# Channel transforms, norms and turns in the Fourier layer of a two-layer encoder, and the place of a small copy in its attention layer

## The chip, the cores and the metric

One core of a Trainium2 chip runs the whole program. The metric is the device time of one execution in microseconds; lower is better. Before the change the median of 3 runs is 1605.82 us (1604.63 to 1607.87).

## The reference

Two token sequences (2048 and 512 rows of 1024 channels, float32) go through the same trunk: an attention layer, a Fourier layer, a final norm.

```python
def attention_layer(x, g, w_in, w_out, sink, rel_bias):
    h = rmsnorm(x, g)
    z = h @ w_in                       # q (16 heads of 64), k and v (4 heads), gate
    ...
    o = banded_gqa_with_sink(q, k, v, rel_bias, sink)   # |i-j| <= 128, bias by distance, a sink logit per head
    return x + (o * jax.nn.silu(gate)) @ w_out

def fourier_layer(x, g, w_gate, w_out):
    h = rmsnorm(x, g)
    hg = h.reshape(b, s, 4, 256)
    f = jnp.fft.fftn(hg, axes=(1, 3), norm="ortho").real   # over positions and the 256 channels of a group
    gate = h @ w_gate
    return x + (f.reshape(b, s, d) * jax.nn.silu(gate)) @ w_out
```

The result is `rmsnorm(x, final_norm)`.

## The kernel before

Products are made in float32 by splitting each operand into a high part (a value in the matmul's reduced format) and a low part (the rest): `matmul3` (line 94 in the profile) issues three matmuls, high by high, high by low, low by high. Where one operand is exact in its high part, two matmuls do. A split is a copy on ScalarE and a subtraction, on VectorE or on POOL. POOL cannot read the matmuls' accumulators (PSUM), so it only works on tiles in SBUF, and does so in pieces of 256 columns.

**Order.** The program is written in Python as straight code; a planner turns it into one fixed list of instructions for each engine, by priority (the order in the program) and by its own estimate of when inputs are ready and buffers free. Each engine then runs its list in order, and waits on semaphores. `seq(engine, ins)` chains instructions of an engine in the order written. Each pool of tiles has a fixed number of buffers (`bufs`), and a tile waits until a buffer is free.

**Attention** (`attention_phase`) runs over five chunks of 512 tokens, in each over eight head pairs `p`, two blocks of 128 queries at a time (17 steps `n`, the work of step `n` overlapping the rest of step `n-1`). In the first chunk the weights are split on the way (lines 113 and 118); later chunks load them split. A head pair's bias tile `bt` has 386 columns: the middle 384 come by a DMA from `rowd` (line 426), the two end columns are the sink logits, copied by ScalarE (line 431). Both are issued in `start()`, at an even step, for the head pair that comes two steps later. `biased` (line 470, VectorE) adds the tile to the scores, `exps` (478, ScalarE) makes the exponentials, `transp` (509) transposes the weights on TensorE, `parts` (517 on ScalarE, 518 on VectorE) splits them, `av` (535) multiplies them with the values, and `out_evac` (544, 553, 555, 558, 559) applies the gate.

**Fourier layer, first part.** Token tiles of 128 rows are taken in ten pairs (`Pair`). For a pair, `load` brings two tiles from memory (line 959), `norms` multiplies each by its inverse root mean square and by the weight `gb` (line 964), where `sumsq` makes the squares on ScalarE (939), the mean on VectorE (87) and the power on POOL (88). `turn` transposes on TensorE: `turn(i, hf)` gives the four blocks of tile `i` with even (`hf` 0) or odd half of each channel group in one PSUM bank, `self.ps[i, hf]`, and mostly splits it (`own`, lines 979 and 980) into `A[i, hf]`. Then two things are computed from a pair.

The gate (`gates`): a product of the 256 tokens with `w_gate` by seven products in place of eight (Strassen's way, Winograd's form), with sums `F[1]` to `F[4]` of the operands (`sums`, lines 995 and 1002), split into `S[1]` to `S[4]` (`parts`, 913 and 914). In order: `W` = A[0,0] B11, `X` by quarters in between, `Z` = S[1] T1, `W` + S[2] T2, `Z` + S[4] B22, `W` + S[3] T3, `W` + A[1,1] N4. Between them stand the reads of the accumulators (`c11`, `c12`, `c22`; VectorE's additions are lines 1105, 1110, 1114), and `hook(0)` to `hook(6)`, where steps of the next pair are put in.

The channel transform, a DFT over the 256 channels of a group, once for each tile of a pair. For tile 1 (`z_odd_even`, line 1036) the table's symmetry is used: even outputs need the sum of the two halves of a group, which is `F[1]`, odd ones their difference, made in PSUM by `odd` (line 986). So a group takes two contractions of 128 rows with 128 columns of the table; both parts of the table stand side by side, so that a matmul has 256 columns: 16 matmuls, evacuated by ScalarE (1043) and VectorE (1044), which adds the two parts. For tile 0 (`z`, `matmul3` at line 94) the whole table is used: 24 matmuls of 256 columns in two banks, evacuated by ScalarE (1022). After every second pair `combine` runs six sums over the four tiles, a radix-4 step over positions (`radix4`, line 1135, VectorE, both operands in SBUF), and POOL stores the results (1198); they are made while the next pair's products run.

Before the first pair the weights `T1`, `T2`, `B11`, `B22` are split and its tiles normalised, between the last steps of the attention layer; `build` splits `N4` and `T3` after its transforms. Buffers: the tag `x` has 4 (one holds the table `chan_sb` throughout; the others serve the tiles `x1`, the sums `F` by twos, and `c`), the tag `hT` 8 (the splits), PSUM 5 banks `bank` (transposes and transforms) and 3 `acc` (products).

**Second part.** The DFT over positions, the gate, the output product (`Outs`, also by seven products, with weights `T1`, `T2`, `T3`, `N4`), and the final norm. For each of the last three frequencies `split_g` is called after the first product and `transform` after the second.

## Time and profile before

| | us |
|---|---|
| median of 3 runs | 1605.82 |
| the runs | 1604.63 to 1607.87 |
| the profiled execution | 1608.11 |
| its span | 1606.3 |
| busy: TensorE | 1586.9 |
| busy: VectorE | 1141.7 |
| busy: ScalarE | 880.3 |
| busy: POOL | 438.2 |

The attention layer lasts until 1076 us, the pairs of the Fourier layer from there to about 1345 us, the second part to the end. PE is TensorE's matmuls, PEld its weight loads, DVE is VectorE, ACT ScalarE, SP the engine that issues most DMAs. A row of a timeline gives the start, the duration, engine, line, operation, output and inputs, count, and in brackets the idle time before it and what ended that. A row of groups ends in busy time, mean nanoseconds of one, and idle time before it. A row of waits gives the engine and line that waited, for whom, the total, the count and the longest. A row of windows gives the length, then the busy time of PE, PEld, DVE, ACT and POOL with the number of instructions, the granted clock, the share of the DMA engines and GB/s.

### The profile page before, as it was taken

What the parts mean: (1) busy time and instruction counts of PE and PEld (TensorE: products, weight loads), DVE (VectorE), ACT (ScalarE), POOL (GpSimd) and SP (SyncE); (2) the same over time, 40 slices, a digit from 0 to 9 for tenths busy, and PEclk for the clock granted to TensorE, in tenths of its full rate; (3) what the DMA queues carried; (4) which work ended last, traced back from release to release, by engine and by line L of the source; (5) the groups of instructions that cost most, each with busy time, mean ns of one, the idle gap of its engine ahead of it and who ended that gap; (6) DMA issues with size and microseconds to landing.
All of it is one profiled execution on the core that took longest, in us unless ns stands there. A gap on an engine that the chain in (4) does not pass through costs nothing.

```text
span 1606.3 us, 27426 instructions
## 1 busy us (share of the span) xinstructions
PE 1586.9 (99%) x9755; PEld 1322.6 (82%) x9755; DVE 1141.7 (71%) x2779; ACT 880.3 (55%) x2107; POOL 438.2 (27%) x605
## 2 busy tenths in 40 slices
PE   9999999999999999999999999999999999999998
PEld 7776888888898888988888888878888887888886
DVE  6787665777538776377764577668878877888696
ACT  6687634677237674257752476646655554343352
POOL 2466561421403414024222242211112121100010
PEclk9999999999999999999999999999999999999999
DMA  7577696655765576756659656656657569455952
GB/s 291 207 286 263 226 349 233 227 220 205 289 230 191 206 257 235 251 194 229 238 164 334 211 208 222 243 201 225 217 203 248 184 224 407 166 185 206 352 192 92
DMA packets 100580, 373.90 MB, mean 233 GB/s; under 512 B 12139, under 2 KB 22379, under 8 KB 83036
## 3 DMA queue, kind: packets, MB, share of 16 engines
q1 hardware_dynamic: 81708, 297.91, 52.4%
q0 software_dynamic: 16400, 70.04, 11.3%
q10 hardware_dynamic: 2336, 4.20, 0.7%
q8 instruction: 78, 1.28, 0.3%
q14 instruction: 58, 0.48, 0.1%
HBM read 280.84 MB, written 91.26 MB: 232 GB/s over the span
## 4 chain that ended last, share of the span: by engine, by line
PE 83%; DMA 7%; DVE 5%; ACT 2%; issue 1%; POOL 1%; SPq 0%; POOLq 0%; DVEq 0%; ACTq 0%
PE qp L94 13%; PE gp L94 12%; PE op L94 9%; PE spt L94 8%; PE spt L451 6%; PE av L535 6%; PE W L94 5%; PE fo L94 4%; PE vp L94 4%; PE pt L509 3%; PE Z L94 3%; PE Wo L94 2%; PE X L94 1%; PE z L94 1%; DMA b<-rowd 1%
## 5 line engine op out<-in xcount | busy, mean ns | idle before, releaser
L470 DVE CUSTOM_DVE_ANT_0 S<-spt,b 128x385 f32<-128x385 f32 (+1 forms) x315 | 154.2, 528 | 121.1 <-PE spt L451 120.8
L94 PE MATMUL qp<-h,wq 128*128 128x512 f32 x960 | 238.6, 398 | 0.0
L94 PE MATMUL gp<-h,wg 128*128 128x512 f32 x960 | 237.4, 395 | 0.0
L94 PEld LDWEIGHTS gp<-h,wg 128*128 128x128 f32 x960 | 174.9, 188 | 43.3 <-issue 9.7
L94 PEld LDWEIGHTS qp<-h,wq 128*128 128x128 f32 x960 | 175.9, 189 | 41.8 <-issue 5.5
L478 ACT ACTIVATE S<-S 128x385 f32<-128x385 f32 (+1 forms) x320 | 190.3, 606 | 18.4 <-DVE S L470 17.0
L517 ACT CAST pts<-pt 128x384 fp32r<-128x384 f32 (+1 forms) x320 | 123.8, 472 | 131.1 <-PE pt L509 130.8
L518 DVE TENSOR_TENSOR pts<-pt,pts 128x384 fp32r<-128x384 f32 (+1 forms) x320 | 147.6, 523 | 34.5 <-ACT pts L517 33.6
L94 PE MATMUL op<-wo,uT 128*128 128x512 f32 x600 | 140.4, 391 | 0.0
L94 PE MATMUL fo<-wo,tTu 128*128 128x512 f32 x576 | 139.1, 392 | 0.0
L94 PEld LDWEIGHTS op<-wo,uT 128*128 128x128 f32 x600 | 111.9, 188 | 23.9 <-issue 0.7
L451 PE MATMUL spt<-kwin,qab 64*128 64x384 f32 (+1 forms) x945 | 129.5, 356 | 0.0
L559 POOL TENSOR_TENSOR uT<-o,uT 128x256 fp32r<-128x256 f32 x75 | 55.6, 741 | 250.5 <-ACT uT L558 246.2
L94 PEld LDWEIGHTS fo<-wo,tTu 128*128 128x128 f32 x576 | 106.3, 188 | 20.3
L535 PEld LDWEIGHTS av<-pts,v 128*128 128x128 f32 x576 | 101.0, 188 | 24.0 <-ACT pts L517 3.7
L535 PE MATMUL av<-pts,v 128*128 128x512 f32 (+1 forms) x576 | 117.0, 342 | 3.3 <-ACT pts L517 2.6
L451 PEld LDWEIGHTS spt<-kwin,qab 64*128 64x128 f32 x945 | 84.2, 185 | 29.9 <-issue 21.5
L490 DVE TENSOR_SCALAR S<-S 128x384 f32<-128x384 f32 (+1 forms) x192 | 91.4, 476 | 6.4
L555 POOL TENSOR_TENSOR o<-o,s 128x256 f32<-128x256 f32 x75 | 55.3, 738 | 134.4 <-DVE o L553 134.1
L94 PE MATMUL spt<-wo,uT 128*128 128x512 f32 x360 | 86.7, 392 | 0.0
L94 PEld LDWEIGHTS spt<-wo,uT 128*128 128x128 f32 x360 | 66.5, 188 | 13.7
L509 PEld LDWEIGHTS pt<-ident,S 64*128 64x128 f32 x1792 | 68.2, 138 | 5.2 <-issue 2.3
(317 smaller groups left out, 2985.8 us busy)
## 6 DMA issues: line engine op xcount, KB each, us to landing
wo<-wsd SPq DMA_DIRECT2D x32, 1024.0 KB, 5.9
wq<-wsd SPq DMA_DIRECT2D x31, 1024.0 KB, 7.6
wg<-wsd SPq DMA_DIRECT2D x31, 1024.0 KB, 5.1
x<-x1d SPq DMA_DIRECT2D x40, 512.0 KB, 3.7
b<-b21d SPq DMA_DIRECT2D x40, 512.0 KB, 6.5
b<-rowd SPq DMA_DIRECT2D x40, 384.0 KB, 4.3
xs<-in_x_dram SPq DMA_DIRECT2D x23, 512.0 KB, 6.7
s2d<-gt POOLq DMA_DIRECT2D x40, 256.0 KB, 3.2
```

Source lines behind the costliest of these rows:

```text
L94: pe(PE.matmul(out, a[i], b[j], start=start and i + j == 0, stop=stop and i == 1, skip_group_check=more))
L451: pe(PE.matmul(banks[j][:, 2 + k0 * P : 2 + k1 * P], res["q"][rows, qp, b * P : (b + 1) * P], kwin[g][rows, kp, b * P + k0 * P : b * P + k ...
L470: seq(DVE, DVE.tensor_tensor_reduce(out=s[:, e0:e1], in0=ps[:, 1 + e0 : 1 + e1], in1=st["bias"][:, j, 386 - e1 : 386 - e0][:, ::-1], scale ...
L478: last_exp[0] = seq(ACT, ACT.activation(s[:, e0:e1], s[:, e0:e1], AF.Exp, bias=s[:, 386:387], scale=-1.0, accum_out=s[:, 387:388]))
L490: seq(DVE, DVE.tensor_scalar(s[:, ks], s[:, ks], den, None, ALU.mult))
L509: pe(PE.transpose(ps[h][:, kb, j, :], ss[j][rows, 1 + kb * P : 1 + (kb + 1) * P], ident[rows, rows]))
L517: seq(ACT, ACT.copy(hi, ps[:, k0:k1]))
L518: seq(DVE, DVE.tensor_tensor(lo, ps[:, k0:k1], f32(hi), ALU.subtract))
L535: pe(PE.matmul(to, v, pt, start=n == part == 0, stop=part == 1 and n in (1, len(todo) - 1), skip_group_check=n > 1,))
L555: eng.tensor_tensor(o, o, s, ALU.mult)
L559: low = eng.tensor_tensor(lo, o, f32(hi), ALU.subtract)
```

## The change

Four things, and a small fifth.

- Both tiles of a pair are transformed the even and odd way (`z(i)`, first tile 1, then tile 0). For tile 0 the new `mix(0)` makes the sum of its two halves (`both`, in the free half of the pair's buffer of sums), splits it into `M[0, 0]` on ScalarE and POOL, and makes the difference in PSUM, split by `own` into `M[0, 1]`. `mix(1)` is what `odd` was. The table is kept for one half of the rows only.
- `norms` scales on ScalarE and multiplies by the weight on POOL in four pieces, in place of one instruction on VectorE.
- The turns of the next pair are put in a product later: `turns1` after the third product, `turns2` after the fourth, `turns3` and `turns4` after the fifth.
- The end columns of the bias tile are copied in a step of their own, `sinks()`, at the end of the odd step before the head pair's first.
- The loads of `N4` in the second part are issued in `transform`, not in `split_g`.

```diff
                     st["bias"] = bt
...
+                def sinks():
+                    ends = ACT.copy(
+                        st["bias"][:, :, 0:386:385], sk[:, 2 * p : 2 * p + 2, None].to_broadcast([P, 2, 2])
+                    )
+                    if p:
+                        seq(ACT, ends)
...
                 at[0].start()
+                at[0].sinks()
...
                     for i in range(4 * n, 4 * n + 4):
                         extra(i)
+                    if n % 2 and n < 15:
+                        at[n // 2 + 1].sinks()
...
                 def norms(self, i):
                     xt = self.x[i]
                     inv = sumsq(xt, f"b{self.ts[i]}")
-                    DVE.scalar_tensor_tensor(xt, xt, inv[:, 0:1], gb, ALU.mult, ALU.mult)
+                    ACT.activation(xt, xt, AF.Copy, scale=inv[:, 0:1])
+                    for j in range(4):
+                        cs = slice(j * 256, j * 256 + 256)
+                        POOL.tensor_tensor(xt[:, cs], xt[:, cs], gb[:, cs], ALU.mult)
...
-                def odd(self):
-                    ps = self.ps[1, 1]
-                    DVE.scalar_tensor_tensor(ps, ps, -2.0, self.F[1], ALU.mult, ALU.add)
-                    self.diff = self.own(ps, f"d{self.n}")
+                def mix(self, i):
+                    ps = self.ps[i, 1]
+                    if i:
+                        both = self.F[1]
+                    else:
+                        both = self.pair[:, 1]
+                        ACT.copy(both, self.ps[0, 0])
+                        DVE.tensor_tensor(both, both, ps, ALU.add)
+                        t = htile([P, 2, 512], F32R, f"tM{self.n}")
+                        ACT.copy(t[:, 0], both)
+                        for j in range(2):
+                            cs = slice(j * 256, j * 256 + 256)
+                            POOL.tensor_tensor(t[:, 1, cs], both[:, cs], f32(t[:, 0, cs]), ALU.subtract)
+                        self.M[0, 0] = t[:, 0], t[:, 1]
+                    DVE.scalar_tensor_tensor(ps, ps, -2.0, both, ALU.mult, ALU.add)
+                    self.M[i, 1] = self.own(ps, f"d{self.n}_{i}")
...
-                def z(self, hf):
-                    ...
-                            matmul3(
-                                ps[:, gg * 256 : gg * 256 + 256], (a[0][:, gs], a[1][:, gs]),
-                                (ch[:, kk, 0], ch[:, kk, 1]), kk == 0, kk == 1,
-                            )
-                    ...
-                def z_odd_even(self):
-                    t = self.ts[1]
+                def z(self, i):
+                    t = self.ts[i]
                     ...
                     for g in range(4):
                         ps = bank(f"z{t}_{g}")
-                        for odd, m in enumerate((self.S[1], self.diff)):
+                        for odd in range(2):
+                            m = self.M[i, odd]
                             to = ps[:, odd * 256 : odd * 256 + 256].rearrange("p (a n) -> p a n", a=2)
                             for part in range(2):
                                 PE.matmul(
-                                    to, m[part][:, g * P : (g + 1) * P], ch[:, 0, :, odd * P : (odd + 1) * P],
+                                    to, m[part][:, g * P : (g + 1) * P], ch[:, :, odd * P : (odd + 1) * P],
                                     start=part == 0, stop=part == 1,
                                 )
...
             def turns2(pr):
                 ...
                 pr.sums(4)
+                pr.mix(0)
                 pr.parts(2)
...
                 gates(pr, {
-                    1: [lambda: turns1(nx)], 2: [lambda: turns2(nx)], 3: [lambda: turns3(nx)], 4: [lambda: turns4(nx)],
-                    5: [lambda: nx.z_odd_even()],
-                    6: [lambda: nx.z(0), lambda: nx.z(1), lambda: combine(nx)],
+                    2: [lambda: turns1(nx)], 3: [lambda: turns2(nx)], 4: [lambda: turns3(nx), lambda: turns4(nx)],
+                    5: [lambda: nx.z(1)],
+                    6: [lambda: nx.z(0), lambda: combine(nx)],
                 })
...
                 def split_g():
                     nxt["s"] = [gated(name, r, xtile) for r in tiles]
-                    if not ft["N4"]:
-                        f_sums("N4", left)
                     nxt["p"] = [halves_of(name, *gl, hf) for hf in range(2)]
...
                 def transform(third):
+                    if not ft["N4"]:
+                        f_sums("N4", left)
```

More of the change, by code (lines that the diff above doesn't have):

```diff
@@ L429, in start @@
                     )
-                    ends = ACT.copy(bt[:, :, 0:386:385], sk[:, 2 * p : 2 * p + 2, None].to_broadcast([P, 2, 2]))
-                    if p:
-                        seq(ACT, ends)
                     st["bias"] = bt
@@ L565, in out_evac @@
                     return split
-                return start, scores, biased, exps, divide, transp, parts, av, out_evac
+                return start, sinks, scores, biased, exps, divide, transp, parts, av, out_evac
             def out_proj(c, uTs):
@@ L628, in out_proj @@
                 return steps
-            Heads = namedtuple("Heads", "start scores biased exps divide transp parts av out_evac")
+            Heads = namedtuple("Heads", "start sinks scores biased exps divide transp parts av out_evac")
             def pieces(out, a, b, op):
@@ L727, in even_odd @@
                 def even_odd():
-                    t = ready["chan"] = xtile([P, 2, 2, 256], F32R, "chan_sb")
+                    t = ready["chan"] = xtile([P, 2, 256], F32R, "chan_sb")
                     src = ready["table"].rearrange("p (a n o) -> p o a n", a=2, o=2)
-                    for kk in range(2):
-                        for odd in range(2):
-                            seq(ACT, ACT.activation(
-                                t[:, kk, :, odd * P : (odd + 1) * P], src[:, odd], AF.Copy, scale=-1.0 if kk and odd else 1.0
-                            ))
+                    for odd in range(2):
+                        seq(ACT, ACT.copy(t[:, :, odd * P : (odd + 1) * P], src[:, odd]))
                 def rows(i):
@@ L1170, in turns1 @@
                 pr.sums(1)
-                pr.odd()
+                pr.mix(1)
             def turns2(pr):
@@ L1611, in split_g, with transform @@
                     nxt["s"] = [gated(name, r, xtile) for r in tiles]
+                    nxt["p"] = [halves_of(name, *gl, hf) for hf in range(2)]
+                def transform(third):
                     if not ft["N4"]:
                         f_sums("N4", left)
-                    nxt["p"] = [halves_of(name, *gl, hf) for hf in range(2)]
-                def transform(third):
                     nxt["o"] = Outs(k1, position(name, k1, None, None, tiles, (nxt["s"], tb), nxt["p"], third))
```

26 lines of the change are left out of this document (8 added, 18 removed).

## The prediction

> **What bounds the kernel now.** I read the page first (busy times, then the 40 slices), after it the timeline of TensorE in the stretch that the change touches, the waits, and the busy time by windows.
>
> ```profile
> PE 1586.9 (99%) x9755; PEld 1322.6 (82%) x9755; DVE 1141.7 (71%) x2779; ACT 880.3 (55%) x2107; POOL 438.2 (27%) x605
> ```
>
> TensorE is busy almost throughout, but such a busy time also covers stretched matmuls, so I look at starts. Here is one pair of the Fourier layer, products and channel transforms:
>
> ```profile
> 1156.58 0.40 PE L1036 MATMUL z<-chan_sb,S 128*128 128x256 f32 x2
> ...
> 1158.49 2.91 PE L94 MATMUL W<-wN,tTb 128*128 128x512 f32 x12
> 1161.24 3.04 PE L94 MATMUL z<-chan_sb,tTb 128*128 128x256 f32 x24
> 1164.11 2.91 PE L94 MATMUL W<-wB,tTb 128*128 128x512 f32 x12
> ```
>
> A product of 12 matmuls takes 1161.24 - 1158.49 = 2.75 us from start to start, 0.23 us a matmul. The second tile's transform (line 1036, 16 matmuls) takes 1158.49 - 1156.58 = 1.91, the first tile's (line 94, 24 matmuls) 1164.11 - 1161.24 = 2.87; both are 0.12 us a matmul. TensorE's whole waiting from 1139 to 1320 us, seven pairs, is one row:
>
> ```profile
> PE z L94 <- DVE z L1044: 0.3, 1, 0.3
> ```
>
> So this stretch is bound by what TensorE issues, and a matmul less there is time less as long as the other engines keep up. How near they are (first window: the first two pairs; second: a pair without the sums of the radix-4 step, line 1135; third: one with them):
>
> ```profile
> core 0: us, PE busy (x) PEld busy (x) DVE busy (x) ACT busy (x) POOL busy (x), PEclk, DMA share, GB/s
> 1076.00:1113.20 37.20, 34.97 (x199) 30.50 (x198) 31.57 (x55) 26.09 (x51) 4.52 (x9) 0.95 0.70 242
> 1138.40:1164.10 25.70, 25.70 (x142) 22.25 (x141) 18.76 (x33) 14.95 (x29) 4.62 (x9) 1.00 0.55 197
> 1164.10:1190.40 26.30, 25.95 (x143) 22.30 (x142) 23.50 (x34) 13.79 (x27) 5.35 (x10) 1.00 0.76 267
> ```
>
> VectorE is the second in line: 2.8 us free in a radix pair, 6.9 in the other, and full at the start, where TensorE idles about 2 us.
>
> **Part 1, transforms.** The first tile's 24 matmuls become 16, as the second tile's are already: 2.87 - 1.91 = 0.96 us less in each of 10 pairs, **-9.6 us**, all on the engine that sets the end.
>
> What the others pay for it, and for the moved norms, by these rows:
>
> ```profile
> L964 DVE SCALAR_TENSOR_TENSOR x<-x,invb,g1b 128x1024 f32<-128x1024 f32 x16 | 20.5, 1284 | 8.3 <-POOL invb L88 7.7
> L939 ACT ACTIVATE jkb<-x 128x1024 bf16<-128x1024 f32 x16 | 16.9, 1056 | 9.9 <-DMA x<-x1d 9.9
> ...
> L1044 DVE SCALAR_TENSOR_TENSOR z<-z,z 128x256 f32<-128x256 f32 x32 | 11.5, 416 | 0.0
> L1002 DVE TENSOR_TENSOR s<-trb,s 128x512 f32<-128x512 f32 x16 | 10.9, 682 | 0.0
> ...
> L995 ACT COPY s<-trb 128x512 f32<-128x512 f32 x16 | 9.7, 608 | 0.2 <-PE trb L972 0.2
> L986 DVE SCALAR_TENSOR_TENSOR trb<-trb,s 128x512 f32<-128x512 f32 x8 | 5.6, 699 | 0.2
> ```
>
> ```profile
> L637 POOL TENSOR_TENSOR e<-w32e,e 128x256 fp32r<-128x256 f32 x48 | 34.4, 738 | 33.1 <-ACT e L693 33.1
> ```
>
> VectorE, per pair: two norm multiplies go (-2.57); the even-odd mix of the first tile brings an add (0.68), a subtract in PSUM (0.70) and the low part of the difference (about 0.69), and four evacuations (4 x 0.42 = 1.66): net +1.16. A radix pair then has 24.7 of 25.3 us, the other 19.9 of 24.7. ScalarE: two scalings of about 1.06, three copies of about 0.61 and 0.3 for smaller evacuations, +4.2 on 14.4: not a bound. POOL: 8 multiply pieces and 2 subtract pieces of 0.74, +7.4 on 5. So by busy time alone everything fits under TensorE's shorter pair. I cost it at nothing there, and price separately what the order and the ports can do.
>
> **Part 2, norms and turns.** A tile's norm loses a 1.28 us step and gains 1.06 (ScalarE) and four pieces, 4 x 0.74 = 2.95 us: 2.7 us longer. Its transposes move one product (2.75 us) back, which pays for exactly that. But the loads of the next tiles wait for buffers that the turns free, so they come 2.7 us later, and the second one up to 3.4 us more, since the mix holds its buffer (ScalarE 0.61, VectorE 0.68, ScalarE 0.61, POOL 1.5). The rows of a radix pair and the pair before it:
>
> ```profile
> 1156.10 0.69 DVE L1110 TENSOR_TENSOR c<-c,W 128x512 f32<-128x512 f32 x1 [0.45 <-PE W L94]
> ...
> 1163.91 1.28 DVE L964 SCALAR_TENSOR_TENSOR x<-x,invb,g1b 128x1024 f32<-128x1024 f32 x1
> 1165.10 1.22 DVE L1135 TENSOR_TENSOR er<-z,z 128x1024 f32<-128x1024 f32 x1
> ...
> 1170.26 1.03 PE L972 MATMUL trb<-ident,x 128*128 128x128 f32 x8
> 1171.39 1.23 DVE L1135 TENSOR_TENSOR er<-er,z 128x1024 f32<-128x1024 f32 x1
> 1173.88 1.03 PE L972 MATMUL trb<-ident,x 128*128 128x128 f32 x8
> ```
>
> The later tile's norm ends at 1165.19 and its transposes are at 1173.88: 8.7 us of slack, of which 8.7 - 2.7 - 3.4 - 2.7 + 2.75 = 2.6 is left. Enough, if POOL isn't held up. That is the doubt: the 8 multiply pieces now fall just where VectorE does the six 1.22 us sums of line 1135 (1165.10 to 1172.62), and both read two operands from SBUF. What then happens is seen where line 211 (VectorE, two SBUF operands) meets POOL's line 206:
>
> ```profile
> 422.52 6.65 POOL L206 TENSOR_TENSOR xk<-xk,invb 128x640 f32<-128x640 f32 x4
> ...
> 424.87 1.28 DVE L211 SCALAR_TENSOR_TENSOR h<-xk,g0s,h 128x512 fp32r<-128x512 f32 x1 [3.21 <-ACT h L210]
> ...
> 429.90 0.74 DVE L211 SCALAR_TENSOR_TENSOR h<-xk,g0s,h 128x512 fp32r<-128x512 f32 x1
> ```
>
> ```profile
> 637.99 6.15 POOL L206 TENSOR_TENSOR xk<-xk,invb 128x640 f32<-128x640 f32 x4
> 640.36 4.34 DVE L211 SCALAR_TENSOR_TENSOR h<-xk,g0s,h 128x512 fp32r<-128x512 f32 x1 [3.02 <-ACT h L210]
> ```
>
> The same instruction takes 0.74 us beside an idle POOL, 1.28 when it gets in after the POOL instruction under way, and 4.34 when POOL's row of four runs through. I take the milder case, which is the commoner in the trace: each sum waits for one piece, 6 x 0.74 = 4.4 us on VectorE. Of this, 1.5 is covered because the turns come later: the last sum ends at 1172.62, the new turn would be at 1170.26 + 2.75 and wants VectorE about 1.1 later, at 1174.1. Another 1.7 is covered because the sum of line 1110 ends at 1156.79 and the product that overwrites what it reads starts at 1158.49. What comes through is 4.4 - 1.5 - 1.7 = 1.2 us, in the four radix pairs that also have norms: **+4.8 us**. Bounds: nothing, or the 24 us of the second rival.
>
> On this the Trainium skill, "SBUF — State Buffer", section "Who interferes with whom", says that VectorE with two SBUF inputs and a POOL instruction that reads SBUF exclude each other for a whole instruction, and that the loser waits rather than slows. By that rule a sum waits for one piece and the term is the 4.8 above; the 4.34 row shows more than one instruction's wait, so there the measurement decides.
>
> **Part 3, the first two pairs.** VectorE is full there: 31.57 busy in a window in which TensorE stands still for about 2 us. Two mixes and eight evacuations bring 2 x 2.07 + 8 x 0.42 = 7.5 us, two norms take off 2.6: 36.5 us of work in 37.2 - 1.9 = 35.3. So the 1.9 saved is not had in full: **+1.6 us** (1.2, and 0.4 as an estimate for pieces that meet two-operand splits; between 0 and 4).
>
> **Part 4, sink columns.** ScalarE writes the end columns of the bias tile behind the bias load, which it overlaps, and waits:
>
> ```profile
> ACT b L431 <- DMA b<-rowd: 55.6, 32, 4.5
> ```
>
> Queued behind it are the casts of the transposed weights (line 517), which TensorE's product with the values needs. Mostly TensorE has other work. In the first chunk twice it has not:
>
> ```profile
> 132.54 0.51 PE L535 MATMUL av<-pts,v 128*128 128x512 f32 x1 [0.81 <-ACT pts L517]
> ...
> 134.36 2.89 PE L94 MATMUL qp<-h,wq 128*128 128x512 f32 x12
> ...
> 139.07 0.56 PE L509 MATMUL pt<-ident,S 64*128 64x64 f32 x11 [0.80 <-DVE o L553]
> ...
> 151.10 0.20 ACT L431 COPY b<-sk 128x4 f32<-128x4 f32 x1 [4.49 <-DMA b<-rowd]
> ...
> 153.73 0.50 PE L535 MATMUL av<-pts,v 128*128 128x512 f32 x1 [1.82 <-ACT pts L517]
> ...
> 155.55 4.49 PE L94 MATMUL qp<-h,wq 128*128 128x512 f32 x12
> ```
>
> ```profile
> 155.50:159.50 4.00, 4.00 (x13) 3.14 (x13) 3.46 (x12) 3.54 (x9) 2.28 (x4) 0.57 0.82 219
> ```
>
> After the second wait the granted clock is 0.57, and twelve matmuls take 4.49 us, not 2.89. Issued a step later, the copy finds its data there and waits for nothing; it is 0.2 us on ScalarE, ahead of the next bias add on VectorE, which waits for scores anyway. The gain is 0.81 + 0.80 + 1.82 + 1.60 = **-5.0 us**; between 0 (a weight load holds ScalarE instead) and 5.6 (two 0.28 us gaps more).
>
> **Part 5, the N4 weights.** Their loads move behind the third layer's gathers; one wait there could go:
>
> ```profile
> PE tr L1337 <- DVE up L1294: 1.2, 1, 1.2
> ```
>
> SyncE was idle when they were issued, so their place need not change: 0, at best -1.2.
>
> **Sum.** 1608.1 (the profiled execution) - 9.6 + 4.8 + 1.6 - 5.0 = 1599.9. It lies 2.3 above the median shown, so 1597.6, -0.5%.
>
> **The rivals.** *All cover holds* (nothing for the ports, nothing at the start, N4's wait gone): 1608.1 - 9.6 - 5.0 - 1.2 = 1592.3, as a median 1590. For it: the free time in the pairs without radix sums. Against: 0.6 us of VectorE left in the others.
>
> *POOL starves VectorE* (slower). As at 640 us, the sums wait out whole bursts: 8 x 0.74 = 5.9 us, and 1.5 more as the mix's two pieces hold up splits. Less the cover of 3.2, TensorE waits 4.2 us before the product of line 1110's bank, more than the wait of 1.82 that cost a further 1.6 in clock: 5.8, in four pairs 23 us. 1608.1 - 9.6 - 5.0 + 1.6 + 23 = 1618, as a median 1616. It decides the sign from 3.3 us lost in each of the four (13.0 / 4). Against it: pieces of 0.74 leave more seams than line 206's of 1.6.
>
> *VectorE becomes the bound*: mix and evacuations come late for the first tile's transform and the pair stays at 25.7 us; only the sinks are gained, 1608.1 - 5.0 + 1.6 = 1604.7, as a median 1602.4.
>
> **How the numbers follow.** Forecast 0.42 (by itself 1592 to 1604), all cover 0.17, starved 0.26, VectorE-bound 0.15. A measurement of this kernel tells 0.2% (3.2 us) from no change. Faster by more: 0.40 + 0.17 + 0.06 = 0.63; slower: 0.24; within: 0.13. Range 1589 to 1614: from just under the best case into the starved one, leaving out its upper part.
>
> **What would show it.** Right: 16 transform matmuls of 1.91 us for both tiles; radix pairs near 26 us, the others 24.7; no wait on the bias load in ScalarE's waits, no clock of 0.57 at 155 us. The sums of line 1135 show the ports: 1.22 us each (cover), about 2 (forecast), over 3 (starved). Wrong: transposes that wait for POOL, or pairs at 25.7 with TensorE waiting on line 1044's evacuation.

## The result and the profile after

The changed kernel takes 1646.46 us (median of 4 runs, 1644.75 to 1648.33) against 1605.58 of the kernel before in the same comparison: ratio 1.0253 (95% interval 1.0235 to 1.0270), slower by 2.5%. The forecast was 1597.6, with 1614 as its upper end. The profiled span is 1644.8 us against 1606.3.

The page's busy times after:

```profile
PE 1599.1 (97%) x9675; PEld 1320.8 (80%) x9675; DVE 1158.8 (70%) x2829; ACT 919.1 (56%) x2175; POOL 528.8 (32%) x705
```

Of the 38.5 us more, TensorE stands idle for 26.3 (1644.8 - 1599.1 against 1606.3 - 1586.9) and is "busy" for 12.2 more, with 80 matmuls fewer. Part of that is the granted clock, 0.990 on average against 0.997: by estimate 0.007 x 1599.1, some 11 us. No other engine is full. Lengths read from the trace (attention chunks from the first product with the value weights to the next; pairs from the first matmul of `Z` = S[1] T1 to the next; in the pairs marked r the radix sums run; the next column goes on from the last such matmul to the first output product `Wo` of the second part; the tail from there to the start of the last matmul):

| | chunk 0, 1, 2, 3, 4 | first two pairs | the eight pairs after them (r first, then every second) | to the first `Wo` | tail |
|---|---|---|---|---|---|
| before | 219.0 214.0 215.0 212.1 196.7 | 40.2 | 25.7r 25.7 26.3r 25.7 25.7r 25.7 25.7r 25.7 | 184.3 | 92.1 |
| after | 215.3 216.0 219.0 218.2 197.4 | 44.5 | 31.5r 25.8 32.7r 25.9 30.9r 26.2 31.7r 25.4 | 186.4 | 91.2 |

So attention loses 9.1 us: the first chunk gains 3.7, the others lose 12.8. The stretch from its end to the first `Wo` loses 30.5, of which the four radix pairs alone lose 23.4. The transforms are 16 matmuls each as foreseen. The windows of the first two pairs, one radix pair and the next pair (columns as before):

```profile
1084.80:1129.30 44.50, 37.81 (x199) 30.81 (x198) 37.17 (x66) 32.82 (x66) 15.41 (x21) 0.96 0.59 200
1245.20:1276.10 30.90, 27.24 (x134) 22.33 (x133) 25.36 (x38) 18.14 (x35) 16.56 (x19) 0.94 0.58 201
1276.10:1302.30 26.20, 25.49 (x134) 21.18 (x133) 18.10 (x36) 18.52 (x35) 11.17 (x18) 1.00 0.45 164
```

In the radix pair TensorE idles 3.7 us and its clock is 0.94; VectorE is busy 25.4 of 30.9 us, so it is not full there. TensorE's waits that are new:

```profile
PE trb L979 <- POOL x L971: 20.5, 24, 2.1
PE spt L455 <- DVE S L474: 5.2, 3, 2.4
PE z L1040 <- ACT s L1015: 2.5, 4, 0.9
```

The first row is the case that the prediction named as wrong: transposes that wait for POOL. The radix pair's start, rows of all engines:

```profile
1244.67 0.14 DVE L87 TENSOR_SCALAR invb<-ssb 128x1 f32<-128x1 f32 x1
1244.79 1.23 DVE L1139 TENSOR_TENSOR er<-z,z 128x1024 f32<-128x1024 f32 x1
...
1246.78 1.14 ACT L968 ACTIVATE x<-x,invb 128x1024 f32<-128x1024 f32 x1
...
1246.97 4.16 DVE L1139 TENSOR_TENSOR z<-z,z 128x1024 f32<-128x1024 f32 x3
...
1248.58 4.79 POOL L971 TENSOR_TENSOR x<-x,g1b 128x256 f32<-128x256 f32 x3
...
1251.16 1.63 DVE L1139 TENSOR_TENSOR z<-er,z 128x1024 f32<-128x1024 f32 x1
...
1251.77 0.33 PE L979 MATMUL trb<-ident,x 128*128 128x128 f32 x1 [0.86 <-POOL x L971]
1252.83 1.63 DVE L1139 TENSOR_TENSOR er<-er,z 128x1024 f32<-128x1024 f32 x1
...
1253.43 0.33 PE L979 MATMUL trb<-ident,x 128*128 128x128 f32 x1 [1.33 <-POOL x L971]
1253.94 3.16 POOL L971 TENSOR_TENSOR x<-x,g1b 128x256 f32<-128x256 f32 x4
...
1255.09 0.87 PE L979 MATMUL trb<-ident,x 128*128 128x128 f32 x5 [1.34 <-POOL x L971]
...
1257.04 3.85 PE L94 MATMUL Z<-wB,S 128*128 128x512 f32 x12
```

Three pieces take 4.79 us beside the sums, 1.6 each; the four at 1253.94, most of them after the last sum, 0.79 each. The last three of the six sums take 1.63 to 1.65 in place of 1.22. Each piece releases one transpose, so the transposes come 1.66 us apart (1251.77, 1253.43, 1255.09) and TensorE waits 0.86 to 1.34 for each; then twelve matmuls take 3.85 us, not 2.88.

Attention, third stall of its kind (the others are at 364 and 580 us):

```profile
800.36 1.06 ACT L161 ACTIVATE xs<-xs 128x1024 f32<-128x1024 f32 x1 [3.25 <-DMA xs<-in_x_dram]
...
801.41 0.18 ACT L437 COPY b<-sk 128x4 f32<-128x4 f32 x1
801.62 0.56 DVE L474 CUSTOM_DVE_ANT_0 S<-spt,b 128x385 f32<-128x385 f32 x1 [4.61 <-ACT b L437]
...
802.24 1.32 PE L455 MATMUL spt<-kwin,qab 64*128 64x384 f32 x5 [2.43 <-DVE S L474]
```

ScalarE waits 3.25 us for the load of a later chunk's rows (line 161, the next chunk's squares, issued by the same step's `extra`); the moved copy is queued behind it, the bias add waits 4.61 us for the copy, and TensorE's scores wait for a bank. Before, a copy stood behind such a wait too:

```profile
796.98 1.06 ACT L161 ACTIVATE xs<-xs 128x1024 f32<-128x1024 f32 x1 [2.36 <-DMA xs<-in_x_dram]
...
798.03 0.18 ACT L431 COPY b<-sk 128x4 f32<-128x4 f32 x1
```

But it was made two steps ahead, and no bias add waited for it. Now it comes just before the step that needs it.

### The profile page after: what moved, and what is told of

The parts are those of the page before. It is cut to its first block, busy times and chain, and to the rows that moved or that the text cites. A ratio compares the mean times of both kernels' runs of the same rounds, so it can differ in the third digit from the quotient of the medians.

```text
span 1644.8 us, 27523 instructions
## 1 busy us (share of the span) xinstructions
PE 1599.1 (97%) x9675; PEld 1320.8 (80%) x9675; DVE 1158.8 (70%) x2829; ACT 919.1 (56%) x2175; POOL 528.8 (32%) x705
## 4 chain that ended last, share of the span: by engine, by line
PE 75%; issue 6%; POOL 6%; DMA 5%; DVE 4%; ACT 3%; SPq 0%; POOLq 0%; DVEq 0%; ACTq 0%
PE gp L94 13%; PE qp L94 13%; PE op L94 8%; PE spt L94 8%; PE spt L455 6%; PE av L539 6%; PE fo L94 4%; PE vp L94 4%; PE pt L513 3%; POOL x L971 3%; PE Wo L94 2%; PE W L94 1%; DMA x<-x1d 1%; PE Z L94 1%; DMA xs<-in_x_dram 1%
## 5 line engine op out<-in xcount | busy, mean ns | idle before, releaser
L94 PE MATMUL gp<-h,wg 128*128 128x512 f32 x960 | 241.3, 400 | 0.0
L522 DVE TENSOR_TENSOR pts<-pt,pts 128x384 fp32r<-128x384 f32 (+1 forms) x320 | 147.6, 523 | 23.8 <-ACT pts L521 23.7
L455 PE MATMUL spt<-kwin,qab 64*128 64x384 f32 (+1 forms) x945 | 133.9, 359 | 5.2 <-DVE S L474 5.2
L455 PEld LDWEIGHTS spt<-kwin,qab 64*128 64x128 f32 x945 | 86.3, 186 | 37.2 <-issue 24.3
L971 POOL TENSOR_TENSOR x<-x,g1b 128x256 f32<-128x256 f32 x80 | 71.1, 919 | 5.9 <-ACT x L968 5.8
```

The lines of the kernel that those rows point to most:

```text
L94: pe(PE.matmul(out, a[i], b[j], start=start and i + j == 0, stop=stop and i == 1, skip_group_check=more))
L455: pe(PE.matmul(banks[j][:, 2 + k0 * P : 2 + k1 * P], res["q"][rows, qp, b * P : (b + 1) * P], kwin[g][rows, kp, b * P + k0 * P : b * P + k ...
L522: seq(DVE, DVE.tensor_tensor(lo, ps[:, k0:k1], f32(hi), ALU.subtract))
L971: POOL.tensor_tensor(xt[:, cs], xt[:, cs], gb[:, cs], ALU.mult)
```

## The experiments

Times are medians; each ratio is to the kernel before, run on the same chip (1605.7 to 1607.5). "Fourier" is the time from the first transposition to the first `Wo`, in the profiled execution: 430.4 before, 460.9 changed. Theory: POOL's pieces meet the radix sums and hold up the transposes, and a copy behind a waiting ScalarE holds up the scores. Rivals: VectorE simply has too much to do, or each part costs by itself.

**1. The parts by themselves.**

```diff
 norms back (the changed kernel, but)
-ACT.activation(xt, xt, AF.Copy, scale=inv[:, 0:1])
-for j in range(4): POOL.tensor_tensor(xt[:, cs], xt[:, cs], gb[:, cs], ALU.mult)
+DVE.scalar_tensor_tensor(xt, xt, inv[:, 0:1], gb, ALU.mult, ALU.mult)
 norms alone, sinks alone, even and odd alone, turns alone: the kernel before with that part of the change
 (even and odd alone keeps the later loads of N4 too)
```

Norms back. 

> The changed kernel with the norm multiply back on VectorE (one instruction, no POOL pieces); everything else stays changed. Theory: POOL's multiply pieces and VectorE's six radix sums take turns at a shared way into SBUF, the pieces come late and the transposes wait for them; without the pieces the four radix pairs fall from 31 to 33 us to about 26, the Fourier layer loses about 25 us, and the time is about 1619 us (slower than before only by the attention layer's 8.8 us, less some of the 9.6 us of matmuls). Rival: the second tile's even-odd transform itself (its mix, its evacuations, its banks) or the later turns hold TensorE up; then the pairs stay near 31 us and the time at 1635 us or above.

Norms alone. 

> The kernel before with only the norms moved to ScalarE and POOL; turns stay a product earlier, transforms as before. Theory: the pieces alone are the cost. The transposes stand 2.7 us earlier than in the changed kernel, so a radix pair loses 6 to 9 us, four of them with norms 24 to 36: 1630 to 1642 us, TensorE waiting for POOL in front of the transposes. Rival: without the mix VectorE has room and the pieces cost little: 1605 to 1612 us.

Sinks alone. 

> The kernel before with only the sink columns copied later, as in the change. Theory: in the first chunk 3.9 us are gained, in the next three the copy stands on ScalarE behind a sum of squares that waits for its load, VectorE's bias add waits for the copy, and TensorE's scores for the bias add: +1.9, +4.0 and +6.1 us; 1614 us in all, attention ending 8 to 9 us later than before. Rival: the attention layer's loss comes from another part (the program's order shifts as the Fourier layer changes): then 1601 to 1602 us, the first chunk's gain alone.

Even and odd alone. 

> The kernel before with the even and odd transform of both tiles alone; norms on VectorE, turns and sink columns as before. Theory: 0.96 us a pair is only had where VectorE has room. The pairs without radix sums fall to about 24.8, the radix pairs, with some 27 us of work for VectorE, go to about 27, the first two pairs lose 1 or 2: 1605 to 1609 against 1607. Rival, the forecast's part 1 taken by itself: the shorter transforms are had in all pairs, 24.7 and 25.3, and the time is 1598 to 1600.

Turns alone. 

> The kernel before with the turns a product later and nothing else. Theory: the loads come 2.7 us later and TensorE's transform of tile 1 stands close behind its operands; pairs 25.7 to 26.2, 1608 to 1611. Rival: the later turns cost what the changed kernel loses in its other pairs, 1 us or more in each: 1616 or more.

| | us | ratio [95%] | Fourier | radix pairs | the others |
|---|---|---|---|---|---|
| norms back | 1620.29 | 1.0091 [1.0072, 1.0109] | 437.1 | 26.9 to 27.2 | 25.4 to 25.7 |
| norms alone | 1619.73 | 1.0082 [1.0066, 1.0099] | 440.4 | 26.6 to 29.4 | 25.7 |
| sinks alone | 1613.73 | 1.0041 [1.0027, 1.0055] | 428.4 | 25.7 | 25.7 |
| even and odd alone | 1610.58 | 1.0021 [1.0011, 1.0030] | 432.6 | 25.6 to 27.6 | 24.7 to 26.0 |
| turns alone | 1605.68 | 0.9992 [0.9983, 1.0002] | 430.4 | 25.7 | 25.7 |

Norms back and sinks alone came out as expected, at about 1619 and 1614. The later turns cost nothing, where 1 to 4 us were expected. In the Fourier stretch the even and odd transform costs 2 us, the norms 10; together, with turns as before, they cost 29 (turns back, in experiment 2). The size of attention's loss varies: it is 6.5 us in the profile of the sinks alone, with 4.1 in chunk 3, and 2.6 (norms back) to 9.9 (sums elsewhere, in experiment 4) in those of the other versions with the same copy.

The norms alone were expected to cost more; their trace says why they don't:

```profile
1220.99 2.82 POOL L967 TENSOR_TENSOR x<-x,g1b 128x256 f32<-128x256 f32 x4 [0.58 <-ACT x L964]
1225.61 4.79 POOL L967 TENSOR_TENSOR x<-x,g1b 128x256 f32<-128x256 f32 x4 [0.71 <-ACT x L964]
1226.56 1.56 DVE L1138 TENSOR_TENSOR er<-z,z 128x1024 f32<-128x1024 f32 x1 [3.27 <-ACT z L1025]
```

The first tile's four pieces are over before the sums begin; only the second tile's meet them. In the last three radix pairs TensorE doesn't wait for POOL at all, but 0.6 to 1.4 us for VectorE's sum of line 1113 (1110 before):

```profile
PE W L94 <- DVE c L1113: 2.8, 3, 1.4
```

That is the wait, and about the size, that the prediction gave each radix pair (1.2). Where the norms are back, radix pairs still take 26.9, and there the same wait shows without the norms' pieces, for VectorE's sum before N4's product (line 1111), beside one for an operand sum's copy:

```profile
PE W L94 <- DVE c L1111: 5.2, 5, 1.6
PE z L1037 <- ACT s L1012: 5.0, 9, 1.1
```

**2. Taking the meeting away.** Three versions of the changed kernel: without the six radix sums (this one leaves them out), with the turns where they were, and with the sums called behind the turns.

```diff
-r = radix4(pairs[pr.n - 1].zs + pr.zs, f"r{gi}")      (no radix sums)
+r = pairs[pr.n - 1].zs + pr.zs
-2: turns1, 3: turns2, 4: turns3, turns4               (turns back)
+1: turns1, 2: turns2, 3: turns3, 4: turns4
-6: nx.z(0), combine(nx)                               (sums behind the turns)
+4: turns3(nx), turns4(nx), combine(pr)   6: nx.z(0)
```

> The changed kernel without the six radix sums of every second pair: the four transformed tiles go on as they are (this leaves out that step of the position transform). The POOL pieces, the longer norm chain, the later loads all stay. Theory (turns taken between pieces and sums): the pieces run at 0.74 us each, the waits for POOL before the transposes go, pairs of both kinds last 25 to 26 us, and the time is 1618 to 1622 us. Rival (the norm chain is too long or its load too late, whatever VectorE does): the waits stay and the time is 1640 us or above.

> The changed kernel with one thing undone: the turns of the next pair stand where they stood before (after the second, third, fourth and fifth product). Theory: the multiply pieces of POOL cost so much because the later turns free their buffers later, so the next loads come 22 to 30 us into a radix pair and the pieces meet the six radix sums; with the turns back the loads come near 12 to 18 us, as in the kernel with the norms alone moved, and the radix pairs fall from 31 to 33 us to 27 to 29: about 1625 us. Rival: the pieces meet the sums wherever the turns stand; radix pairs stay at 31 or more and the time at about 1643.

> The changed kernel with the six radix sums called after the turns of the next pair and no longer ahead of them; all work is still done. Theory: the loss is the meeting of POOL's pieces with the sums ahead of the transposes. Behind the turns the sums meet no piece, transposes come 5.4 to 11 us into every pair as without the sums, radix pairs come to 26 to 27: 1622 to 1628 (attention still costs 8.8). Rival: VectorE and POOL have too much to do wherever the sums lie; radix pairs stay at 30 or more and the time is above 1638.

Without the sums: 1614.78 us, ratio 1.0047 [1.0031, 1.0064], Fourier 429.2; the third pair is at 26.4 and all from the fourth on at 24.8 to 25.5, eight pieces and all. That is the time the change meant to have in its pairs:

```profile
1200.80:1225.60 24.80, 24.80 (x133) 21.13 (x132) 17.39 (x33) 18.29 (x35) 11.33 (x19) 1.00 0.59 214
1225.60:1250.50 24.90, 24.90 (x134) 21.15 (x133) 17.40 (x33) 18.43 (x35) 10.28 (x16) 1.00 0.60 213
```

Turns back: 1644.05, 1.0232 [1.0215, 1.0249], radix pairs 30.0 to 31.3: the later turns are not the cause. Sums behind the turns: 1651.16, 1.0271 [1.0254, 1.0288], radix pairs 32.1 to 33.6, against the theory. In its order two of the six sums still lie among the pieces, and the other four stand ahead of VectorE's later steps:

```profile
PE trb L979 <- POOL x L971: 14.7, 23, 2.1
PE z L1040 <- ACT s L1015: 7.1, 9, 1.5
PE W L94 <- ACT c L1093: 5.7, 4, 1.4
```

The six sums can't simply be put elsewhere: the wait on POOL shrinks from 20.5 to 14.7 and two others grow. VectorE is busy for 24.3 of 32.3 us of such a pair, so it isn't full either.

**3. The same pieces where no sums run.** Norms on ScalarE and POOL for odd pairs only (`if self.n % 2`), turns as before; once with the sum of `mix` in the pair's buffer and the sink columns ahead of the step's `extra`, once with the sum in a buffer of its own and the sink columns a step later in the first chunk alone.

> Even and odd transforms for both tiles, turns as before, sink columns ahead of the step's extra work, and the norms on ScalarE and POOL for the odd pairs only, whose tiles are loaded while a radix pair runs and should reach POOL when its six sums are over; the even pairs' norms stay on VectorE. Theory: the pieces meet no radix sum, VectorE is rid of 2.6 us in the radix pairs, so these stay at 25.3 to 26 and the others fall to 24.8: 1596 to 1599. Rival: the pieces still meet VectorE's splits and sums, or POOL's pieces hold up the transposes; radix pairs of 27 or more, 1605 or more.

> As the kernel with own buffer and norms on VectorE, but the norms of odd pairs on ScalarE and POOL. Theory: with the loads of these pairs back at 15 to 18 us into a radix pair, their pieces lie behind the radix sums and ahead of the transposes; VectorE has 2.6 us less in a radix pair; pairs of 24.8 and 25.3, 1597 to 1599. Rival: the pieces still come late (the norm is 2.7 us longer than on VectorE) and TensorE waits for POOL in every second pair, as with odd norms and the shared buffer: pairs of 26.5 or more, 1608 or more.

1626.40, 1.0117 [1.0100, 1.0134], and 1620.92, 1.0088 [1.0071, 1.0105]: the rival both times. The radix pairs are good (25.8 to 26.7; in the second 24.8 to 25.4, but for 27.1 in the first of them), the pairs with POOL's norms are not: 26.7 to 28.9 and 26.8 to 29.7. In the second:

```profile
1147.12 0.15 DVE L87 TENSOR_SCALAR invb<-ssb 128x1 f32<-128x1 f32 x1 [1.26 <-ACT jkb L946]
...
1148.21 5.53 POOL L975 TENSOR_TENSOR x<-x,g1b 128x256 f32<-128x256 f32 x8 [0.24 <-ACT x L972]
...
1148.99 0.33 PE L985 MATMUL trb<-ident,x 128*128 128x128 f32 x1 [0.71 <-POOL x L975]
...
1152.56 0.69 DVE L993 TENSOR_TENSOR tTb<-trb,tTb 128x512 fp32r<-128x512 f32 x1 [5.28 <-ACT tTb L992]
```

Undisturbed, two tiles' pieces take 5.53 us in a row, where VectorE took 2 x 1.28, and VectorE then idles 5.28 us for the transposes. So pieces also cost by their length on the path, without any meeting, where the turns stand as before. In the version without the sums the eight pieces lie at the same place (from about 3 to 8.5 us into a pair) and the turns a product later, and there they cost nothing: the later turns do pay for the longer norm, as the prediction had it. Odd norms with later turns were not run.

**4. Why the tiles are late.** In the changed kernel the loads of the next tiles come 22 to 31 us into a radix pair; before, at 12 and 16 (15 and 20 in the first). Four versions of the changed kernel, and one of a better one, were to bring them forward.

```diff
-both = self.pair[:, 1]                                 (own buffer)
+both = main.tile([P, 512], F32, tag="xr", bufs=3, name=f"both{self.n}")
-pr.sums(4); pr.mix(0); pr.parts(2) ... pr.sums(3); pr.parts(3)           (own buffer and mix last)
+pr.sums(4); pr.parts(2) ... pr.sums(3); pr.parts(3); pr.mix(0)
-self.pair = xtile([P, 2, 512], F32, ...)               (sums elsewhere)
+self.pair = (htile if i == 4 else xtile)([P, 2, 512], F32, ...)
-DVE.tensor_scalar(inv, ss, 1.0 / D, EPS, ...)          (mean on POOL, on top of mix last)
+POOL.tensor_scalar(inv, ss, 1.0 / D, EPS, ...)
```

> The changed kernel with one edit: the sum that mix makes of tile 0 stands in a buffer of its own (a third user of a tag of three half-size buffers) and no longer in the free half of the pair's buffer. Theory: in the changed kernel the third operand sum waits for POOL's two pieces of tM, its low part is what the load of the next pair's second tile waits for, and this tile's pieces then meet the radix sums. With the own buffer the second load comes about 6 us earlier (22 to 24 us into a radix pair and not 28 to 31), more of the eight pieces are done ahead of the sums, radix pairs fall from 31 to 33 us to 28 to 29 and the time to about 1630. Rival: the loads wait for something else; loads and pairs stay and the time is 1643 or more.

> The changed kernel with the sum of mix in a buffer of its own and mix of tile 0 called last, behind the third operand sum and its split. Theory: on ScalarE and VectorE the mix stands ahead of the split whose buffer the second load waits for; called last, loads come 3 to 5 us earlier (about 19 and 25 us into a radix pair), some pieces are done ahead of the sums, and radix pairs fall to about 28 to 29: about 1630. Rival: the lateness comes from the transposes that wait for POOL's pieces, whatever the order behind them; 1643 or more.

> The changed kernel with one word changed: the buffer of the third and fourth operand sums is taken from the eight buffers of the splits and no longer from those that the next tiles are loaded into. Theory (a loop through the buffers): the second load no longer waits for the third sum's split, comes 5 us or more earlier (at most 24 us into a radix pair, 18 into the others), the norm's chain starts earlier and radix pairs fall from 31 to 33 us to 27 to 29; about 1628. Rival: it is the meeting of pieces and radix sums by itself, wherever the load comes, or the splits now wait for their eight buffers; radix pairs stay at 31 or more, 1640 or more.

> The changed kernel with own buffer and mix last (1643.1 us) and one more edit: the mean of the norm's squares on POOL, ahead of the power, and no longer on VectorE. Theory: the norm's chain goes through the lists of four engines, and on VectorE and ScalarE it stands behind the evacuations of both transforms, so that pieces start when the radix sums start. Without VectorE in the chain ScalarE's scaling of the first tile stands ahead of the second transform's evacuations; its four pieces are done before or just as the sums begin, the second tile's transposes come at 10 to 12 us into a radix pair and not at 14 to 15, radix pairs fall from 31.5 to 28 to 29, and the time to 1628 to 1634. Rival: pieces meet the sums wherever the mean is made, radix pairs stay at 31 or more; 1640 or more.

> The version with own buffer, norms on VectorE, turns as before and the sink columns later in the first chunk alone, with mix of tile 0 called last. Theory: second loads come from 19 to 22 us into a pair back to 16 to 18, the pairs of 25.5 and 26.5 us fall to 24.7, and the time to about 1599 to 1601 from 1603.7. Rival: the mix comes too late for the first tile's transform; TensorE waits for its parts, 1606 or more.

| | us | ratio [95%] | loads, us into a radix pair | radix pairs |
|---|---|---|---|---|
| own buffer | 1646.93 | 1.0253 [1.0236, 1.0270] | 23, 29 to 30 | 31.4 to 32.3 |
| mix last | 1643.07 | 1.0232 [1.0215, 1.0249] | 20 to 22, 24 to 26 | 31.2 to 33.2 |
| sums elsewhere | 1669.30 | 1.0380 [1.0354, 1.0406] | 14 to 16, 19 to 27 | 36.7 to 38.9 |
| mean on POOL | 1656.48 | 1.0313 [1.0295, 1.0330] | 22, 25 to 28 | 31.2 to 36.0 |
| vector norms, mix last | 1611.86 | 1.0035 [1.0022, 1.0049] | 14 to 16, 19 to 21 | 25.5 to 27.3 |

All five theories fell by their times. With the sums elsewhere the loads ahead of a radix pair come 11 and 15 us into the pair before it, as in the kernel before, and still the pieces begin 2.5 to 4.2 us into the radix pair:

```profile
1245.20 4.70 SPq L963 DMA_DIRECT2D x<-x1d  x2
1248.40 1.06 ACT L943 ACTIVATE jkb<-x 128x1024 bf16<-128x1024 f32 x1 [0.71 <-DVE s L1022]
...
1259.48 0.20 DVE L87 TENSOR_SCALAR invb<-ssb 128x1 f32<-128x1 f32 x2
1259.78 2.72 POOL L88 TENSOR_TENSOR invb<-invb,mhalf 128x1 f32<-128x1 f32 x2 [0.70 <-DVE invb L87]
1261.28 2.41 ACT L968 ACTIVATE x<-x,invb 128x1024 f32<-128x1024 f32 x2 [1.15 <-POOL invb L88]
1262.51 3.12 POOL L971 TENSOR_TENSOR x<-x,g1b 128x256 f32<-128x256 f32 x2
```

The squares are there at 1249.5, their mean, 0.1 us of VectorE's work, comes at 1259.48: in VectorE's list it stands behind the mix and the evacuations of both transforms. The norm's chain goes through ScalarE, VectorE, POOL, ScalarE and POOL, each with a fixed list. TensorE's longer wait in this version is another, though: 4.8 to 6.7 us in each radix pair for an operand sum's copy (line 1015), beside 2.5 to 3.1 for POOL. With the mean on POOL the first tile's four pieces do run ahead of the sums in the last three radix pairs (the last of them at 1.6 to 2.1 us into the pair, the first sum at 2.2 to 2.7), and the wait on POOL falls to 5.0 us, all of it in the first radix pair. But ScalarE's scaling of the second tile now waits for POOL, and the copy of the first product's accumulator is queued behind it:

```profile
PE W L94 <- ACT c L1094: 18.3, 7, 4.4
PE trb L979 <- POOL x L971: 5.0, 7, 1.3
```

In the profiles this version's tail is 8 us longer than that of mix last (100.5 against 92.6), which lies outside the pairs and the theory; that the radix pairs stay above 31 us is what speaks against it.

**5. Sink columns.** In the kernel before, `sinks()` called ahead of the step's `extra` work, not behind it:

```diff
+if n % 2 and n < 15:
+    at[n // 2 + 1].sinks()
 for i in range(4 * n, 4 * n + 4):
     extra(i)
```

> The kernel before with the sink columns alone moved, but called ahead of the step's extra work and not behind it. Theory: the moved copy lost time in chunks 1 to 3 because on ScalarE it stood behind a Square that waits for its load, and the bias add waits for the copy; ahead of it, chunk 0 keeps its gain of about 4 us, chunks 1 to 3 stay at 214, 215 and 212, and the time is 1602 to 1603. Rival: any place at the end of an odd step holds up a bias add; chunks 1 to 3 are again 2 to 4 us longer, 1611 to 1614.

1607.61, ratio 0.9996 [0.9986, 1.0006], between the theory and the rival. Chunks 214.2 214.4 215.7 212.7 197.4: the stalls of chunks 1 to 3 are gone and the first chunk is shorter. But in the profiled execution it also begins 2.4 us later (21.4 us against 19.1) and the later chunks are each 0.4 to 0.7 us longer, so attention ends where it did, at 1075.9. With the copy at the same place in the first version of experiment 3 the first chunk begins at 19.2 and attention ends 1.0 us earlier. I have not traced either, and the median shows no gain.

**6. Towards a better version.** Sink columns a step later in the first chunk alone (`if c == 0`), norms on VectorE, turns as before, own buffer; then the even and odd transform for both tiles in all pairs, or for tile 0 in odd pairs alone, whose mix runs beside no radix sum:

```diff
+if pr.n % 2:
+    pr.mix0()
-6: nx.z(0), nx.z(1), combine(nx)
+6: nx.z_odd_even(0) if nx.n % 2 else nx.z(0), nx.z(1)   7: combine(nx)
```

> Even and odd transform of both tiles with the sum in a buffer of its own, norms on VectorE, turns as before, and the sink columns a step later in the first chunk alone. Theory: second loads come back from 19 to 22 us into a pair to 16 to 18, the pairs without radix sums are all at 24.7, radix pairs at 25.3 to 25.6, the first chunk gains 4.8 and chunks 1 to 4 lose nothing: 1599 to 1601. Rival: VectorE is the bound and the buffer changes nothing; pairs as in the even and odd transform alone, only the sinks are gained: 1605 to 1606.

> The kernel before with tile 0 transformed the even and odd way in odd pairs alone, whose mix falls beside no radix sum (the sum in a buffer of its own), norms and turns as before, sink columns a step later in the first chunk alone. Theory: four or five pairs become 0.96 us shorter, since VectorE has 6.9 us free there, radix pairs stay at 25.7, and the first chunk gains 4.8: 1598 to 1600. Rival: the mix delays the loads of the next pair, which then come late for the radix pair, and the gain is given back: 1602 to 1604.

All pairs: 1603.67, 0.9979 [0.9967, 0.9990], short of the theory: the second loads still come 18.7 to 23.2 us into the pairs, not 16 to 18, so the buffer is not what they mostly wait for. Odd pairs alone: **1599.81, 0.9951 [0.9934, 0.9967]**, the fastest, as expected. In its profile chunk 0 takes 215.9 us, the others as before but for 0.7 in chunk 3, and the stretch to the first `Wo` is 1.6 longer, which I have not traced; two neighbouring pairs, without a wait of TensorE from 1139 to 1320 us:

```profile
1190.30:1215.00 24.70, 24.70 (x134) 21.27 (x133) 19.86 (x35) 15.88 (x33) 5.11 (x7) 1.00 0.44 153
1215.00:1240.60 25.60, 25.60 (x141) 22.20 (x140) 21.52 (x34) 14.26 (x28) 5.74 (x10) 1.00 0.75 261
```

The matmuls saved are had in full where VectorE has room.

## Why the prediction was wrong

By place, the profiled execution at 1646.7 against the 1599.9 of the sum: the four radix pairs together were to take 1.0 us more (4 x (1.2 - 0.96)) and took 23.4; attention was to gain 5.0 and lost 9.1; the first two pairs -0.3 and +4.3; the other four pairs -3.8 and +0.5; the stretch to `Wo` 0 and +2.1; the tail 0 and -0.9. So two steps failed above all, part 2 and part 4.

- **Part 1 (-9.6).** "By busy time alone everything fits" was the error. Alone, the even and odd transform gave +2.2 in the Fourier part. The mix's operations stand in the queues ahead of the third operand sum and of the next norm: the second load comes at 22 us into a radix pair, not 16. An own buffer for the sum gets 3.4 us of this back (429.2 against 432.6), though the second loads stay at 21.6 to 23.2 us into the radix pairs; odd pairs alone get their full microsecond each.
- **Part 2 (+4.8): the step that failed, in size and in place.** The slack of 8.7 us was charged with 2.7 for one tile's norm and 3.4 for the mix. The mix took 6.4 (loads from 15.6 to 22.0), so nothing was left; and POOL's eight pieces are one row of 5.5 us undisturbed and lie over some 11 in a radix pair (1248.58 to 1259.45): 8.9 of their own, the rest POOL's issues of stores of the radix results between them, which this part of the sum left out. "Enough, if POOL isn't held up" was the right doubt, but I priced it on the wrong engine: I let each sum wait for a piece, on VectorE, while in each radix pair three pieces lost 0.7 to 1.0 us each and three sums 0.4, and TensorE's transposes waited for the pieces, 20.5 us (some 14 of it in the four radix pairs), with the lower clock behind them.
- The Trainium skill, "SBUF — State Buffer", section "Who interferes with whom", has a VectorE instruction with two SBUF inputs and a POOL instruction that reads SBUF exclude each other for a whole one. A sum and a piece in turn would take 1.22 + 0.74 = 1.96 us by that. The trace looks like turns, but of 1.66 (a piece ends 0.58 us after each of the last three sums, at 1251.71, 1253.37 and 1255.04), so the two overlap a little and the measurement decides.
- **The turns** are right: a product later costs nothing by itself, and pays for the longer norm where no sums run (experiment 3).
- **Part 3.** Two mixes and eight evacuations into a full VectorE: predicted -0.3 for the first two pairs net, measured +4.3 (44.5 against 40.2), of which the transforms alone give +1.8 and the norms alone +3.0. There too TensorE's transposes wait for POOL's pieces, 4.2 us.
- **Part 4 (-5.0): the other step that failed, in sign.** ScalarE's wait for the bias load falls from 55.6 to 7.6 us, the first chunk gains 3.7, the wait of 1.82 and the clock of 0.57 at 155 us are gone; in their place the same product waits 1.38 us at 141.8. But "waits for nothing" and "waits for scores anyway" were only looked at in that chunk. In chunks 1 to 3 the copy stands behind a ScalarE instruction that waits for a load, and the bias add needs it at once: +2.0, +4.0, +6.1.
- **Part 5** fits: TensorE's wait of 1.2 is down to 0.2, and the tail is 0.9 shorter. It was not run by itself.
- **The rivals.** The slower one had the sign and POOL as its cause, but its 1616 is 30 short, and VectorE was not starved: the sums took 1.22 to 1.65, with one of 2.37, not over 3. VectorE as the bound at 25.7 us describes the even and odd transform alone (25.6 to 25.8 in three of the four radix pairs).

Shown: more than half of the loss of 30.5 us (29 - 10 - 2 = 17) comes only where the new transform and POOL's norms stand together, and in the changed kernel all of it goes with the radix sums. Without the norms on POOL 23.8 us come back, without the sums 31.7, and the transform turns the norms' 10 into 29. VectorE's load is not the cause: with the norms back on it, it has 2.6 us more to do in a pair, and the radix pairs fall from 31 to 33 us to 27. Not shown is that the meeting of pieces and sums costs TensorE as much wherever it lies: called behind the turns, only two sums still lie among the pieces, and the radix pairs take no less. Open: which single order of the lists would let the pieces run ahead of the sums with no other wait; of the attempts with the sums behind the turns, the mix last, the sums elsewhere and the mean on POOL, each left the wait on POOL or put another in its place.

## What to carry to other kernels

A step taken off a busy engine and spread over others is costed by the length of its new chain and by its place in each engine's fixed list, not by busy time: here 1.3 us on VectorE became 4 us through ScalarE and POOL, and in one version a 0.1 us mean stood 10 us in a queue. Two moves that each fit into the same slack don't fit together, so charge them to it in one sum. Where a part pays only in some iterations, make it only there, and before calling a moved copy free, look in every chunk for what stands ahead of it on its engine and how soon its result is needed.

## What was not expected of the hardware

POOL's multiply pieces went from 0.74 to between 1.46 and 1.71 us beside VectorE's two-operand sums, and those from 1.22 to 1.63: the loss is on both, and the larger share on POOL. A power of one element per partition (line 88) took 1.40 and 1.47 us there, and 0.55 elsewhere. And behind three waits of 0.9 to 1.3 us in a row the granted clock was lower (0.66, then 0.75), with twelve matmuls in 3.85 us in place of 2.88; the windows around them in the changed kernel, granted clock in the third column from the end:

```profile
1251.00:1255.00 4.00, 0.66 (x2) 0.28 (x2) 3.39 (x3) 0.42 (x1) 3.98 (x4) 1.00 0.14 56
1255.00:1257.00 2.00, 1.91 (x8) 1.66 (x9) 0.38 (x1) 1.00 (x2) 2.00 (x4) 0.66 0.37 150
1257.00:1261.00 4.00, 4.00 (x16) 3.18 (x15) 1.68 (x4) 1.28 (x3) 2.43 (x5) 0.75 0.84 196
```
